# First two weight chunks issued from ScalarE's queue; squares of the first norm later; the eighth square kept beside the sum

## The chip, the cores and the metric

The kernel runs on one core of one Trainium2 chip. The metric is the device time of one execution in microseconds (us), from outside the program; the profile's span, from the first to the last instruction, is a little shorter. Each engine (TensorE = PE, with its weight loads listed apart as PEld; VectorE = DVE; ScalarE = ACT; GpSimd = POOL; SyncE = SP) runs its own list of instructions in order and waits on semaphores for the others. DMA queues are fed by an issuing instruction on an engine; in the kernel before, all of them stand on SP.

## What is computed

Two layers of a decoder trunk on 256 tokens of width 1024, float32. Each layer normalises x, multiplies it with one wide matrix, runs three token mixers, merges them through gates, and ends with a gated feed-forward block behind a second norm:

```python
def _rms(x, g):
    y = xf * lax.rsqrt(jnp.mean(xf * xf, axis=-1, keepdims=True) + EPS)
    return (y * g.astype(jnp.float32)).astype(x.dtype)

xn = _rms(x, norm_mix_g);  z = jnp.einsum('btd,dc->btc', xn, w_in)
...                        # mLSTM, sparse attention, differential attention, branch gates
x = x + jnp.einsum('btd,de->bte', merged, w_out)
xn = _rms(x, norm_ffn_g);  gu = jnp.einsum('btd,df->btf', xn, w_gate_up)
return x + jnp.einsum('btf,fd->btd', jax.nn.silu(g) * u, w_down)
```

So there are four norms in a run: the mixing norm and the feed-forward norm of each of the two layers. The first of them opens the program.

## The kernel before, in words

**Tiling.** x is held transposed: 8 blocks `x[0]` to `x[7]` of 128 features by 256 tokens, side by side in the tile `xs` (lines 485 and 486). Weights come in chunks of 128 by 1024 (`chunk`, lines 509 to 522), numbered here c0, c1, c2, ... in the order of use. A chunk is loaded into one of three `raw` buffers and split: ScalarE writes the rounded high part `whi`, VectorE the rest `wlo` (`split`, lines 524 to 526); three buffers each. The activations are split in the same way (`gained`, line 547, gives `xg` or `fx`). A product is then three matmul passes, hi by hi, hi by lo and lo by hi (`feat`, line 528), each with 256 columns; one chunk is 24 matmuls. A `raw` buffer is free for a next load when its `wlo` is done, so the load of c7 waits for the `wlo` of c4.

**Start.** The first layer's first two chunks and x are loaded in pieces (lines 602 to 620): x in four pieces of two blocks, c0 and c1 in halves of 512 columns, all eight from SP, alternating. `x_parts` splits the blocks, `split` the halves. `first_pair` (line 630) runs 26 small matmuls on zeros and then the 48 matmuls of c0 and c1 in the order in which pieces become ready. Then c2, c3, ... follow in full chunks.

**Norm.** Matmuls run on `x * gain`; the factor 1/rms is applied afterwards to what the matmuls gave. `norm` (line 551) computes it: the squares of the eight blocks are summed in `acc` (tile `nacc`); PE transposes `acc` (tokens to partitions), VectorE reduces it to `rcol`, GpSimd takes the power -1/2, VectorE copies it out (`rc`), PE transposes that back and ScalarE writes it as `rB`. In the first norm (lines 566 to 573) the squares are two ScalarE instructions of 1024 columns, held behind the `wlo` of c1 in the planned order (line 568), and three VectorE additions. In the other three (lines 575 to 581) each block is squared by ScalarE and added by GpSimd, 7 additions one after the other. What a matmul of the first layer left in PSUM is read out as `pad` (line 792), which needs `rB`; until then the PSUM buffer is held.

**Order.** The code records all operations, and a list scheduler (`Order.schedule`, line 206) with a cost table puts them into one order, per engine; each engine runs its list as it stands. `S.after(view)` holds the next operations in that planning behind the writers of the view. `PLACED` (line 416) lists tiles and spacers that are laid out first in SBUF.

Of the kernel before, what the change touches and what calls it, by code (L numbers as in the profile page):

```python
# [11 lines left out]
F32 = mybir.dt.float32  # L12
F32R = mybir.dt.float32r
BF16 = mybir.dt.bfloat16
AF = mybir.ActivationFunctionType
OP = mybir.AluOpType
AX = mybir.AxisListType.X
# [100 lines left out]
class Order:  # L118
# [87 lines left out]
    def schedule(self):  # L206
        ops = self.ops
# [39 lines left out]
        while len(out) < len(ops):  # L247
            for e in ENGINES:
                if e not in stale:
                    continue  # L250
                c = []
                full = set()
                for p, i in sorted(avail[e]):
                    tag = ops[i].bases[0].tag
                    if tag in full:
                        continue
                    at = start(ops[i], t_eng[e])
                    if at is not None:
                        c.append((at, p, i))
                    if e == "sync":  # L260
                        full.add(tag)
                if c:
                    t = min(c)[0] + SLACK[e]
                    picks[e] = min((p, i, at) for at, p, i in c if at <= t)
                else:
                    picks[e] = None
            stale.clear()
            c = [(picks[e][2], e) for e in ENGINES if picks[e]]
            if not c:
                raise RuntimeError("the order is stuck: " + repr([(e, [(ops[i].fn, [(b.name, b.slot, len(free[b.tag])) for b in ops[i].bases]) for _, i in sorted(avail[e])[:6]]) for e in ENGINES]))  # L270
            at, e = min(c)
            p, i, _ = picks[e]
            o = ops[i]
# [3 lines left out]
            for b in o.bases:  # L277
                if not b.slot:
                    free[b.tag].pop(0)
                    b.slot = True  # L280
                    stale.update(ENGINES)
            if e == "sync":
                dma = max(at, dma) + o.dur
                o.end, t_eng[e] = dma + DMA_LAT, at + DMA_ISSUE
            else:
                if e == "scalar":
                    fits = [f for f in TABLES if o.args[2] in f]
                    if fits and table not in fits:
                        table = fits[0]
                        at += 1.283  # L290
                o.end = t_eng[e] = at + o.dur
# [62 lines left out]
def cost(op, views):  # L354

    n = max(math.prod(v.shape[1:]) for v in views)
    psum = any(v.base.psum for v in views)
    if op.eng == "tensor":
        n = math.prod(views[0].shape[1:])
# [4 lines left out]
        if views[1].dtype == F32R:  # L364
            return max(n, 256) / 2400 + 0.0024
        return 0.216 if n <= 128 else 4 * n / 2400 + 0.0048
    if op.eng == "scalar":
        t = (0.05 if psum else 0.092) + n * 0.00084
        extra = [op.kw.get("scale"), op.kw.get("bias"), op.kw.get("accum_out")]
        return t + 0.093 * sum(isinstance(v, View) for v in extra)  # L370
# [23 lines left out]
T = 256  # L394
# [18 lines left out]
BR = (1, 2, 0)  # L413


PLACED = ("whi", "wlo", "nacc", 192, "xg", "y", "h", 192, "w", 224, "mqk", 192, "K1", 416)


def plan():
# [37 lines left out]
def kernel(ctx: ExitStack, tc: tile.TileContext, xT: bass.AP, wts: bass.AP, cst: bass.AP,  # L457
# [6 lines left out]
    S = Order(tc, sbuf, psum)  # L464
# [5 lines left out]
    def atps(shape):  # L470
        return S.tile(shape, F32, tag="at", name="at", bufs=4, psum=True)

    def tmp(shape, name="w"):
        return S.tile(shape, F32, tag="w", name=name, bufs=NW)
# [76 lines left out]
    def norm(gcol, wide, xg=None):  # L551

        first = xg is not None
        xg = xg or []
        acc = S.tile([128, T], F32, tag="nacc", name="nacc")
        for k in range(8 - len(xg)):
            g = gcol[:, k:k + 1]
            if not wide:
# [6 lines left out]
            xg.append(a)  # L565
        if first:
            sq = S.tile([128, 8 * T], F32, tag="y", name="sq8", bufs=3)
            with S.after(w_first[1][1]):
                for a in (0, 4 * T):
                    A.activation(sq[:, a:a + 4 * T], xs[:, 8 + a:8 + a + 4 * T], AF.Square)  # L570
            for n in (4 * T, 2 * T):
                V.tensor_add(sq[:, 0:n], sq[:, 0:n], sq[:, n:2 * n])
            V.tensor_add(acc, sq[:, 0:T], sq[:, T:2 * T])
        else:
            for k in range(8):
                if k == 0:
                    A.activation(acc, x[k], AF.Square)
                else:
                    sq = tmp([128, T], "nsq")
                    A.activation(sq, x[k], AF.Square)  # L580
                    G.tensor_add(acc, acc, sq)
        ps = atps([128, 2, 128])
        with S.gang():
            for t in range(2):
                PE.transpose(ps[:, t, :], acc[:, t * 128:(t + 1) * 128], ident)
        rcol = S.tile([128, 2], F32, tag="rcol", name="rcol", bufs=2)
        V.tensor_reduce(rcol, ps, axis=AX, op=OP.add)
        V.tensor_scalar(rcol, rcol, 1.0 / D, EPS, op0=OP.mult, op1=OP.add)
        rsqrt_cols(rcol, 2)
        rr = tmp([128, 2, 128], "rc")  # L590
# [11 lines left out]
    xg0, w_first = [], [chunk(0), chunk(0)]  # L602
    with S.early(10 ** 6):
        def load(i, a, b):
            SP.dma_start(w_first[i][0][:, a:b], w_first[i][3][:, a:b])

        def load_x(k, n):
            a = 8 + T * k if k else 0
# [150 lines left out]
                                       op0=OP.mult, op1=OP.subtract)  # L759

    for li in range(L):
        widx[0] = 2 if li == 0 else 0
        c = col[li]
        r = row[li] = S.tile([128, R_N], F32, tag="row", name="row")
        ps_first = mmps([128, 2, T]) if li == 0 else None
        if li == 0:
            first_pair(ps_first)
        xg, rcol, rB = norm(c[:, C_NM:C_NM + 8], False, xg0 if li == 0 else None)
        if li:
            SP.dma_start(r, rows[li:li + 1, :].to_broadcast([128, R_N]))  # L770
# [7 lines left out]
        for fp in range(4):  # L778
            if li == 0 and fp == 0:
                ps = ps_first  # L780
            else:
                ps = mmps([128, 2, T])
                for j in range(2):
                    w = chunk(li)
                    for k in range(8):
                        feat(ps[:, j, :], w, k * 128, xg[k], k == 0, k == 7)
            qk = S.tile([128, 2, T], F32, tag="mqk", name="mqk", bufs=4)
# [496 lines left out]
```

## Time and profile before

| what | value |
|---|---|
| device time, median of 3 runs | 909.11 us (903.57 to 916.03) |
| time of the profiled execution | 910.13 us |
| its span | 908.0 us |
| PE busy | 897.8 us, 7162 matmuls |
| DVE, ACT, POOL busy | 675.6, 536.0, 111.6 us |
| granted TensorE clock | 1.000 |

The profiled execution lies 1.02 us above the median of the three, and its time is 2.1 us more than its span. The first real matmul starts 6.28 us into the span. Of the last 108 us PE is busy for 104.25; what is left is the end of the kernel behind its last matmul, mostly. PE's records are pipelined matmuls that overlap: their durations of some 280 ns are longer than the distance from one to the next.

### The profile page before, as it was taken

Reading aid. Unit: us, or ns where it says so; the run is one execution under the profiler, and the core shown is the slowest. Engines: PE = TensorE matmul, PEld = TensorE weight load, DVE = VectorE, ACT = ScalarE, POOL = GpSimd, SP = SyncE. Lnnn points to the kernel's source line nnn. Section 1 sums busy time; section 2 is a strip of 40 time slices with the busy share of each in tenths; the row PEclk is TensorE's granted clock in tenths of the full one; section 3 lists DMA queues with packets and bytes.
Section 4 is the critical chain, followed back from the end, with each engine's and each line's share of the span. In section 5 each row is a group of like instructions: output and inputs, shape, how many; then the busy total and the mean of one; then the engine's idle time right before and its main releaser. Section 6 shows DMA issues by size and latency. Waiting matters only on the chain.

```text
span 908.0 us, 18059 instructions
## 1 busy us (share of the span) xinstructions
PE 897.8 (99%) x7162; PEld 857.3 (94%) x7162; DVE 675.6 (74%) x1276; ACT 536.0 (59%) x928; POOL 111.6 (12%) x142
## 2 busy tenths in 40 slices
PE   9999999999999999999999999999999999999998
PEld 8978779999999999999999787899999999999998
DVE  6999989766896666665578899897669866666553
ACT  6786677765465444444457857687654655545442
POOL 0333342300021000000110221312000300000000
PEclk9999999999999999999999999999999999999999
DMA  8665524356555555555665554433555555555663
GB/s 260 197 200 183 165 91 126 123 176 196 196 187 186 187 186 187 186 176 189 190 188 181 181 186 141 138 110 125 186 190 194 198 185 191 197 195 189 197 210 102
DMA packets 46453, 160.50 MB, mean 177 GB/s; under 512 B 5408, under 2 KB 6560, under 8 KB 46368
## 3 DMA queue, kind: packets, MB, share of 16 engines
q1 hardware_dynamic: 46368, 159.34, 53.8%
q8 instruction: 56, 0.92, 0.4%
q14 instruction: 29, 0.24, 0.1%
HBM read 158.27 MB, written 1.05 MB: 175 GB/s over the span
## 4 chain that ended last, share of the span: by engine, by line
PE 88%; DVE 6%; POOL 2%; DMA 2%; issue 1%; ACT 1%; ACTq 0%; DVEq 0%
PE mm L323 83%; PE at L323 5%; DVE e L323 2%; DVE wlo L323 2%; POOL s L323 2%; DMA raw<-in_wts_dram 1%; ACT whi L323 1%; DMA x<-in_xT_dram 0%; DVE zr L323 0%; DVE cv L323 0%; DVE y L323 0%; DVE s L323 0%; DVE rot L323 0%; DVE pad L323 0%; DVE xg L323 0%
## 5 line engine op out<-in xcount | busy, mean ns | idle before, releaser
L323 ACT ACTIVATE whi<-raw 128x1024 fp32r<-128x1024 f32 (+3 forms) x304 | 316.5, 1042 | 316.6 <-PE mm L323 150.3
L323 DVE TENSOR_TENSOR wlo<-raw,whi 128x1024 fp32r<-128x1024 f32 (+3 forms) x304 | 364.5, 1200 | 170.8 <-ACT whi L323 169.0
L323 PE MATMUL mm<-fx,whi 128*128 128x256 f32 x1408 | 245.1, 279 | 0.0
L323 PEld LDWEIGHTS mm<-fx,whi 128*128 128x128 f32 x1408 | 214.7, 189 | 0.0
L323 PE MATMUL mm<-fx,wlo 128*128 128x256 f32 x704 | 195.9, 279 | 0.0
L323 PE MATMUL mm<-xg,whi 128*128 128x256 f32 x1024 | 181.4, 280 | 0.3 <-ACT whi L323 0.3
L323 PEld LDWEIGHTS mm<-xg,whi 128*128 128x128 f32 x1024 | 155.4, 188 | 1.7 <-issue 0.7
L323 PE MATMUL mm<-whi,xg 128*128 128x512 f32 (+2 forms) x512 | 149.1, 372 | 1.1 <-DVE pad L323 1.1
L323 PE MATMUL mm<-xg,wlo 128*128 128x256 f32 x512 | 142.5, 281 | 0.8 <-DVE wlo L323 0.8
L323 PEld LDWEIGHTS mm<-fx,wlo 128*128 128x128 f32 x704 | 132.0, 188 | 0.0
L323 PE MATMUL mm<-h,whi 128*128 128x256 f32 x704 | 122.1, 279 | 0.0
L323 PEld LDWEIGHTS mm<-whi,xg 128*128 128x128 f32 x512 | 92.0, 188 | 17.3 <-issue 1.5
L323 PEld LDWEIGHTS mm<-h,whi 128*128 128x128 f32 x704 | 107.4, 189 | 0.0
L323 PE MATMUL mm<-h,wlo 128*128 128x256 f32 x352 | 98.1, 279 | 0.0
L323 PEld LDWEIGHTS mm<-xg,wlo 128*128 128x128 f32 x512 | 95.8, 188 | 1.1 <-DVE wlo L323 1.1
L323 PE MATMUL mm<-wlo,xg 128*128 128x512 f32 (+2 forms) x256 | 94.9, 371 | 0.0
L323 PEld LDWEIGHTS mm<-h,wlo 128*128 128x128 f32 x352 | 66.1, 188 | 0.0
L323 PE MATMUL mm<-y,whi 128*128 128x256 f32 x384 | 65.4, 276 | 0.0
L323 POOL TENSOR_TENSOR nacc<-nacc,nsq 128x256 f32<-128x256 f32 x21 | 20.2, 962 | 348.0 <-ACT nsq L323 210.1
L323 PEld LDWEIGHTS mm<-y,whi 128*128 128x128 f32 x384 | 57.8, 188 | 0.0
L323 PEld LDWEIGHTS mm<-wlo,xg 128*128 128x128 f32 x256 | 48.1, 188 | 7.3
L323 PE MATMUL mm<-y,wlo 128*128 128x256 f32 x192 | 53.0, 276 | 0.0
(199 smaller groups left out, 1083.6 us busy)
## 6 DMA issues: line engine op xcount, KB each, us to landing
raw<-in_wts_dram SPq DMA_DIRECT2D x278, 512.0 KB, 3.4
raw<-in_wts_dram SPq DMA_DIRECT2D x16, 384.0 KB, 3.8
raw<-in_wts_dram SPq DMA_DIRECT2D x4, 498.0 KB, 4.0
raw<-in_wts_dram SPq DMA_DIRECT2D x4, 256.0 KB, 4.8
out_dram<-x SPq DMA_DIRECT2D x8, 128.0 KB, 3.4
row<-in_rows_dram SPq DMA_DIRECT2D x2, 388.0 KB, 5.3
x<-in_xT_dram SPq DMA_DIRECT2D x3, 256.0 KB, 5.0
raw<-in_wts_dram SPq DMA_DIRECT2D x2, 332.0 KB, 3.0
```

What stands on the lines that cost most here:

```text
L323: getattr(getattr(nc, o.eng), o.fn)(*args, **kw)
```

## The change

It does four things. (1) The halves of c0 and c1 are issued from ScalarE's queue (`A.dma_start`), and SP issues x alone; the scheduler is taught that a DMA can stand on another engine than SP. (2) c2 and c3 are declared ahead of the first norm (`w_next`), and the two squares of that norm are planned behind the `whi` of c2 and of c3. (3) `nacc` is now 128 x 2 x 256, a temporary tile; in the first norm the last addition of 256 columns is left out and the addition before it writes `nacc`; in the other three the eighth square is written by ScalarE into the second half, so GpSimd adds 6 times. Four transposes instead of two bring it to the reduction, which runs over 512 columns instead of 256. (4) `nacc` is no longer in `PLACED`, so the tiles behind it lie 1024 bytes lower in each partition.

```diff
-PLACED = ("whi", "wlo", "nacc", 192, "xg", "y", "h", 192, "w", 224, "mqk", 192, "K1", 416)
+PLACED = ("whi", "wlo", 192, "xg", "y", "h", 192, "w", 224, "mqk", 192, "K1", 416)
...
-        acc = S.tile([128, T], F32, tag="nacc", name="nacc")
+        acc = tmp([128, 2, T], "nacc")
...
-            with S.after(w_first[1][1]):
-                for a in (0, 4 * T):
-                    A.activation(sq[:, a:a + 4 * T], xs[:, 8 + a:8 + a + 4 * T], AF.Square)
-            for n in (4 * T, 2 * T):
-                V.tensor_add(sq[:, 0:n], sq[:, 0:n], sq[:, n:2 * n])
-            V.tensor_add(acc, sq[:, 0:T], sq[:, T:2 * T])
+            for a in range(2):
+                with S.after(w_next[a][0]):
+                    A.activation(sq[:, 4 * a * T:4 * (a + 1) * T], xs[:, 8 + 4 * a * T:8 + 4 * (a + 1) * T], AF.Square)
+            V.tensor_add(sq[:, 0:4 * T], sq[:, 0:4 * T], sq[:, 4 * T:8 * T])
+            V.tensor_add(acc.rearrange("p a t -> p (a t)"), sq[:, 0:2 * T], sq[:, 2 * T:4 * T])
         else:
             for k in range(8):
-                if k == 0:
-                    A.activation(acc, x[k], AF.Square)
+                if k in (0, 7):
+                    A.activation(acc[:, k // 7, :], x[k], AF.Square)
                 else:
                     sq = tmp([128, T], "nsq")
                     A.activation(sq, x[k], AF.Square)
-                    G.tensor_add(acc, acc, sq)
+                    G.tensor_add(acc[:, 0, :], acc[:, 0, :], sq)
-        ps = atps([128, 2, 128])
+        ps = atps([128, 2, 2, 128])
         with S.gang():
-            for t in range(2):
-                PE.transpose(ps[:, t, :], acc[:, t * 128:(t + 1) * 128], ident)
+            for i in range(2):
+                for t in range(2):
+                    PE.transpose(ps[:, t, i, :], acc[:, i, t * 128:(t + 1) * 128], ident)
...
-            SP.dma_start(w_first[i][0][:, a:b], w_first[i][3][:, a:b])
+            A.dma_start(w_first[i][0][:, a:b], w_first[i][3][:, a:b])
```

**ScalarE's list at its start**, before and after. `xg` are the high parts of the blocks of x, `whi` those of weights (512 columns: halves of c0 and c1). Before:

```order
L323 ACT_TABLE_LOAD
L323 ACTIVATE warm<-warm 128x1
L323 ACTIVATE xg<-x 128x256 x2
L323 ACTIVATE whi<-raw 128x512
L323 ACTIVATE xg<-x 128x256 x2
L323 ACTIVATE whi<-raw 128x512 x2
L323 ACTIVATE xg<-x 128x256 x2
L323 ACTIVATE whi<-raw 128x512
L323 ACTIVATE xg<-x 128x256 x2
L323 ACTIVATE sq_68<-x 128x1024
L323 ACTIVATE whi<-raw 128x1024
L323 ACTIVATE sq_68<-x 128x1024
```

After:

```order
L323 DMA raw<-in_wts_dram 128x512 x4
L323 ACT_TABLE_LOAD
L323 ACTIVATE warm<-warm 128x1
L323 ACTIVATE whi<-raw 128x512
L323 ACTIVATE xg<-x 128x256 x2
...
L323 ACTIVATE whi<-raw 128x512
L323 ACTIVATE xg<-x 128x256 x2
L323 ACTIVATE whi<-raw 128x1024
L323 ACTIVATE sq_67<-x 128x1024
L323 ACTIVATE whi<-raw 128x1024
L323 ACTIVATE sq_67<-x 128x1024
```

Four DMA issues stand ahead of the table load; each half of a chunk is split ahead of the two blocks of x that it was behind; and each square has moved one whole `whi` back, behind those of c2 and c3.

**VectorE's list around the first norm**, from the `wlo` of c2 on (all `wlo` here are whole chunks, in the order c2, c3, c4, c5). Before:

```order
L323 TENSOR_TENSOR wlo<-raw,whi 128x1024
L323 TENSOR_TENSOR sq_68<-sq_68 128x1024
L323 TENSOR_TENSOR wlo<-raw,whi 128x1024 x2
L323 TENSOR_TENSOR sq_68<-sq_68 128x512
L323 TENSOR_TENSOR nacc<-sq_68 128x256
L323 TENSOR_TENSOR wlo<-raw,whi 128x1024
L323 TENSOR_REDUCE rcol<-at 128x2
```

After:

```order
L323 TENSOR_TENSOR wlo<-raw,whi 128x1024 x2
L323 TENSOR_TENSOR sq_67<-sq_67 128x1024
L323 TENSOR_TENSOR wlo<-raw,whi 128x1024
L323 TENSOR_TENSOR nacc<-sq_67 128x512
L323 TENSOR_TENSOR wlo<-raw,whi 128x1024
L323 TENSOR_REDUCE rcol<-at 128x2
```

The first addition of squares has moved from behind the `wlo` of c2 to behind that of c3, just ahead of that of c4, and one addition is gone.

On PE the transposes of the first norm's `nacc` stand 4 matmuls further back than before (behind the first matmul of c4), those of `rc` 5 matmuls further forward, so that 27 matmuls lie between the two instead of 36. In the two feed-forward norms the transposes of `nacc` stand 7 matmuls further forward, in the mixing norm of layer 1 five. Apart from the four norms and the start, every engine's list is the same, names aside.

## Rows read from the trace of the kernel before

**Rows 1.** Page: the span, and busy time of each engine.
```profile
span 908.0 us, 18059 instructions
PE 897.8 (99%) x7162; PEld 857.3 (94%) x7162; DVE 675.6 (74%) x1276; ACT 536.0 (59%) x928; POOL 111.6 (12%) x142
```

**Rows 2.** Waits of PE: engine and tile, waited for; us in total, times, longest.
```profile
PE at L323 <- DVE zr L323: 2.0, 2, 1.8
PE mm L323 <- DVE pad L323: 1.1, 1, 1.1
PE mm L323 <- DVE wlo L323: 0.8, 1, 0.8
```

**Rows 3.** Chain that ended last, in order of time: start us, us, what.
```profile
10.36 4.63 DMA raw<-in_wts_dram
...
17.46 5.81 DMA raw<-in_wts_dram
...
35.18 20.06 PE mm L323 x114
...
105.96 1.14 PE at L323 x16
```

**Rows 4.** Tile x: SP's issues, ns min/median/max, first and last start.
```profile
L323 SPq DMA_DIRECT2D x<-in_xT_dram x4: 387/428/449, 0.7 to 4.1; - x4
```

**Rows 5.** Windows: length, busy us of engines (count), clock, DMA share, GB/s.
```profile
2.00:3.00 1.00, 1.00 (x7) 0.69 (x6) 0.00 (x0) 0.21 (x2) 0.00 (x0) 1.00 0.67 156
...
5.00:6.00 1.00, 0.95 (x9) 0.59 (x6) 0.66 (x2) 1.00 (x3) 0.00 (x0) 1.00 1.04 399
```

**Rows 6.** Timeline of ScalarE: start, us, operation, count, idle before and its releaser.
```profile
0.72 1.28 ACT L323 ACT_TABLE_LOAD   x1 [0.72 <-PEq L1273]
...
4.79 0.91 ACT L323 ACTIVATE xg<-x 128x256 fp32r<-128x256 f32 x2 [2.57 <-DMA x<-in_xT_dram]
5.61 0.61 ACT L323 ACTIVATE whi<-raw 128x512 fp32r<-128x512 f32 x1
...
11.27 1.05 ACT L323 ACTIVATE whi<-raw 128x1024 fp32r<-128x1024 f32 x1
...
13.51 1.06 ACT L323 ACTIVATE whi<-raw 128x1024 fp32r<-128x1024 f32 x1 [0.24 <-DMA raw<-in_wts_dram]
```

**Rows 7.** Timeline of VectorE, from c2's low part to the first pad.
```profile
12.35 1.22 DVE L323 TENSOR_TENSOR wlo<-raw,whi 128x1024 fp32r<-128x1024 f32 x1 [0.80 <-ACT whi L323]
13.50 1.22 DVE L323 TENSOR_TENSOR sq<-sq 128x1024 f32<-128x1024 f32 x1
...
16.20 1.23 DVE L323 TENSOR_TENSOR wlo<-raw,whi 128x1024 fp32r<-128x1024 f32 x1 [0.35 <-ACT whi L323]
...
18.07 0.42 DVE L323 TENSOR_TENSOR nacc<-sq 128x256 f32<-128x256 f32 x1
...
20.79 0.42 DVE L323 TENSOR_REDUCE rcol<-at 128x2 f32<-128x256 f32 x1
...
25.60 0.42 DVE L323 TENSOR_TENSOR pad<-mm,rB 128x256 f32<-128x256 f32 x1
```

**Rows 8.** Timeline of PE: c2's first low pass, and the first norm's transposes.
```profile
13.63 0.39 PE L323 MATMUL mm<-xg,wlo 128*128 128x256 f32 x1 [0.76 <-DVE wlo L323]
...
18.64 0.38 PE L323 MATMUL at<-K,nacc 128*128 128x128 f32 x2
...
23.51 0.66 PE L323 MATMUL at<-K,rc 128*128 128x128 f32 x4 [0.39 <-DVE rc L323]
```

**Rows 9.** Timeline of PE around a later norm (feed-forward, layer 0).
```profile
277.30 0.44 PE L323 MATMUL at<-K,nacc 128*128 128x128 f32 x2
277.49 0.48 PE L323 MATMUL mm<-fx,whi 128*128 128x256 f32 x2
...
280.99 0.60 PE L323 MATMUL at<-K,rc 128*128 128x128 f32 x4
281.34 0.36 PE L323 MATMUL mm<-fx,whi 128*128 128x256 f32 x1
```

More of the change, by code (lines that the diff above doesn't have):

```diff
@@ L259, in schedule @@
                         c.append((at, p, i))
-                    if e == "sync":
+                    if ops[i].fn == "dma_start":
                         full.add(tag)
@@ L281, in schedule @@
                     stale.update(ENGINES)
-            if e == "sync":
+            if o.fn == "dma_start":
                 dma = max(at, dma) + o.dur
@@ L366, in cost @@
         return 0.216 if n <= 128 else 4 * n / 2400 + 0.0048
-    if op.eng == "scalar":
+    if op.eng == "scalar" and op.fn != "dma_start":
         t = (0.05 if psum else 0.092) + n * 0.00084
@@ L580, in norm @@
                     A.activation(sq, x[k], AF.Square)
-                    G.tensor_add(acc, acc, sq)
-        ps = atps([128, 2, 128])
+                    G.tensor_add(acc[:, 0, :], acc[:, 0, :], sq)
+        ps = atps([128, 2, 2, 128])
         with S.gang():
-            for t in range(2):
-                PE.transpose(ps[:, t, :], acc[:, t * 128:(t + 1) * 128], ident)
+            for i in range(2):
+                for t in range(2):
+                    PE.transpose(ps[:, t, i, :], acc[:, i, t * 128:(t + 1) * 128], ident)
         rcol = S.tile([128, 2], F32, tag="rcol", name="rcol", bufs=2)
-        V.tensor_reduce(rcol, ps, axis=AX, op=OP.add)
+        V.tensor_reduce(rcol, ps.rearrange("p t a c -> p t (a c)"), axis=AX, op=OP.add)
         V.tensor_scalar(rcol, rcol, 1.0 / D, EPS, op0=OP.mult, op1=OP.add)
@@ L761 @@
     for li in range(L):
-        widx[0] = 2 if li == 0 else 0
+        if li:
+            widx[0] = 0
         c = col[li]
@@ L767 @@
             first_pair(ps_first)
+            w_next = [chunk(0), chunk(0)]
         xg, rcol, rB = norm(c[:, C_NM:C_NM + 8], False, xg0 if li == 0 else None)
@@ L783 @@
                 for j in range(2):
-                    w = chunk(li)
+                    w = w_next[j] if li == 0 and fp == 1 else chunk(li)
                     for k in range(8):
```

## The prediction

> **What bounds the kernel now.** I first read the page. TensorE is busy for 897.8 of 908.0 us [rows 1], so all that a better order could ever win is the other 10.2 us, 1.1% of the time. A measurement of this kernel can tell about 2% (18.2 us) from no change, and the three runs of before alone lie 12.5 us apart. No hidden wait can therefore make this kernel faster by 2%: the questions are only which way the few microseconds at the start go, and whether something makes the matmuls themselves slower.
>
> Next I read PE's waits. In the stretch that the change touches there are two: 0.8 us for the `wlo` of c2, which ends at 13.63 [rows 8], and 1.1 us for a `pad`, which ends at 35.18 [rows 2, 3]. The 1.8 us for `zr` comes at 132 us, behind a stretch of VectorE and GpSimd work that PE itself started at 105.96 [rows 2, 3]; a shift of PE at 35.18 goes through to the end of the kernel undiminished.
>
> The chain of waits says which of the two counts. Up to 35.18 it does not run over PE. It runs over loads and splits: the load of c4 (4.63 us from 10.36), c4's split, the load of c7 (5.81 us from 17.46), c7's split, and then VectorE's `pad` [rows 3]. A load of c7 starts when c4's `wlo` is done: 16.20 plus 1.23 is 17.43 [rows 7]. Reading this, a PE that is early at 13.63 only waits longer at 35.18. **The time at 35.18 is set by when VectorE finishes c4's `wlo`.**
>
> **Part 1, the issues.** SP's four x issues run from 0.7 to 4.1 us because four weight issues of a like 0.43 us stand between them [rows 4]. Taken apart, the last of each kind is issued near 2.1, up to 2 us earlier. But the DMA engines are full soon after: 156 GB/s in the third microsecond, 399 in the sixth, with a share of 1.04 [rows 5]. What the earlier issue wins can only be in the ramp. The trace has no second queue, so I bound it. Best case: the first half chunk lands beside x's first piece at 4.79, where ScalarE's wait for x ended. Worst case: the two share the engines and both land when, before, both had landed, which is by 5.61, where ScalarE took the half chunk without a wait [rows 6]. So ScalarE starts between 4.79 and 5.61, that is 0 to 0.8 us later than before.
>
> Here the Trainium skill speaks against the change: "DMA: Bandwidth & Descriptors", section "Issuing engines are not separate DMA queues", says that DMAs from several engines run on the same 16 DMA engines and interleave, and that only the sequencer's issue time is saved; its section on queues, rings and completion order has each DMA engine go round between queues packet by packet. By that rule the first piece of x lands together with the first half chunk, the late case. The saturated row agrees; the sharing itself no run here shows.
>
> The four issues on ScalarE take some 4 x 0.43 = 1.7 us (SP's price; ScalarE's is not in the trace). With the 1.28 us table load behind them ScalarE is ready near 0.72 + 1.7 + 1.28 = 3.7, before anything lands [rows 4, 6]. They cost nothing; if an issue took twice as long, ScalarE would be ready at 5.4 and they would cost up to 0.6.
>
> **Part 2, the new order at the start.** ScalarE does the same 12 instructions (8 blocks, 4 halves) until the last block. Before, c2's `whi` came at 11.27 because a square of 1.05 us stood ahead of it [rows 6]; now it starts at 10.3 to 11.1. c2's `wlo` then ends 0.1 to 0.9 us earlier than 13.57, and so PE's wait of 0.76 shrinks to 0 to 0.7. This is what the move of the squares gives.
>
> **Part 3, what the squares run into.** They now follow the `whi` of c2 and c3, and VectorE's first addition of them, 1.22 us, has moved to just ahead of c4's `wlo` [rows 7]. c3's `whi` starts on its load, at 13.51 [rows 6], and ends at 14.57; the second square ends near 15.6, and c4's `whi` near 16.6. On VectorE c3's `wlo` ends at 14.6 + 1.2 = 15.8, the addition, waiting for the square, at 17.0, c4's `wlo` at 18.2. Before it ended at 17.43: **c4's `wlo` is 0.8 us later**, 1.4 at most if the pieces land late. Behind it on VectorE wait the sum, c5's `wlo` and the reduction; on SP waits the load of c7.
>
> **Part 4, the sum and its way back.** One addition of 512 columns writes `nacc`; its 0.69 us is between the 0.42 us of 256 columns and the 1.22 of 1024 [rows 7]. `nacc` is ready at 18.9 where it was at 18.49. Before, 43 matmuls lay between 13.63 and 18.64 [rows 8], 0.117 us each; PE would now want it 47 after 12.7 to 13.5, at 18.2 to 19.0, so a new wait of up to 0.8 us is likely there. Then c5's `wlo` (1.2) and the reduction over twice the columns (0.42, up to 0.84): 20.8. From the reduction's start to the transposes of `rc` it took 23.51 - 20.79 = 2.7 us [rows 7, 8]; now 20.2 + 2.7 + 0.2 = 23.1. PE comes there after 27 instead of 36 matmuls, at 19.0 + 0.45 + 3.15 = 22.6, and waits 0.5 us (0.39 before). It has then done 5 fewer matmuls (0.6 us) 0.4 us earlier: 0.2 us behind, which the 1.1 us of slack in front of 35.18 covers.
>
> **Part 5, at 35.18.** c7's load starts near 18.2. With the two latencies of the chain, 4.63 and 5.81 [rows 3], it lands at 22.8 to 24.0; before, at 23.27. In the middle that is 0.15 later; with the late start (18.8) and the long latency, 1.4 later. It can't help more than some 0.9: `rc` at 23.1 still has to become `rB` before the first `pad`, which stood at 25.60 [rows 7] behind c7's `wlo`. I take +0.3, from -0.9 to +1.4.
>
> **Part 6, the three later norms.** There PE is the bound. Two transposes took 0.19 us until the next matmul, four 0.35 [rows 9]: +0.16 each, 0.5 us together, 0.3 if transposes that come without a short wait for GpSimd's sum are cheaper. GpSimd's missing addition and the earlier sum win nothing, since no wait of PE in the table of waits stands there [rows 2].
>
> **The sum.** 910.13 + 0.3 + 0.5 = 910.9 for a profiled execution, with bounds -0.6 and +1.9. The profiled execution of before lies 1.02 above the median, so the median comes to 909.9 us. It is a shift of less than 0.1%, far inside the scatter of the runs.
>
> **The rivals.**
>
> *A, the start pays.* The two queues fill the ramp, c7's load takes the short latency, and `pad` comes up to 0.9 us earlier: 910.13 - 0.9 + 0.3 is 909.5, a median of 908.5. For it speaks the row of 156 GB/s; against it, that c4's `wlo` would have to keep its time despite the addition put in front.
>
> *B, the late start.* x shares the engines with the weights, everything at the start is 0.8 us later, c4's `wlo` ends at 18.8 and `pad` is 1.4 late: 910.13 + 1.4 + 0.5 = 912.0, a median of 911.0. This is what the page's interleaving makes of it. For it speaks the share of 1.04 [rows 5], against it that the engines are not full before the fifth microsecond.
>
> *C, slower by more than 2%: the new places in SBUF.* All tiles behind `wlo` move by 1024 bytes. If TensorE's reads depended on that, 18.2 us over 7162 matmuls is 2.5 ns each, from 0.117 to 0.1195 us; from there on it decides. It would be seen in every stage, not at the start, and the time would be 928 us or more. Against it: VectorE's splits of c2 and c4, in different buffers of each of the three kinds, took 1.22 and 1.23 us [rows 7], so the address did not show there.
>
> That the change does nothing at all is part of the forecast: the loads are hidden or bound by bandwidth, and the time does not move.
>
> **How the numbers follow.** The forecast (a shift at the end between -0.5 and +1.5 us) has 0.56, A 0.2, B 0.2, C 0.03, and 0.01 stays for a gain of 2% that no row explains. A and B end within 2% as the forecast does. So: faster 0.01, same 0.96, slower 0.03. The cases A to B span only 908.5 to 911.0; the runs of before scatter from 5.5 below to 6.9 above their median, and a new median will share in that. The range goes from 903.5 (A and a scatter of 5) to 916.0 (B and a scatter of 5).
>
> **What the changed profile would show.** Right: ScalarE idle until its first `whi` at 4.8 to 5.6; c2's `wlo` ends before 13.5; the addition of squares stands between c3's and c4's `wlo` and c4's ends near 18.2; PE waits for `nacc`, at about 19; the wait for `pad` near 35 has grown to 1.0 to 2.5 us; the first matmul behind it starts between 34.3 and 36.6; four transposes at each later norm. Wrong: if the whole of PE's steady stretch (300 to 400 us, no idle) has another number of matmuls per microsecond, it is C. If the matmul behind `pad` starts before 34.3, the chain of loads was not what I took it for. If there is a wait of PE of over 1 us at a later norm, part 6 falls.

## The result, and the profile after

The changed kernel takes 903.46 us (median of 21 runs, 902.74 to 904.49) against 909.65 us (902.23 to 916.91) of the kernel before beside it: medians 6.2 us apart, 0.7%. The ratio is 0.995, 95% interval 0.9933 to 0.9967; it and all ratios below leave out executions that are over 1.5% longer than the fastest of their kernel, here the five longest of before. The forecast was 909.9 us, between 903.5 and 916.0. The ratio is below one beyond its interval, and the forecast had no such gain in it.

The single times say more than the medians. The 21 runs of before lie on three levels: six at 902.2 to 903.6, nine at 908.8 to 910.7, six at 915.2 to 916.9. Nothing lies between the levels, which are some 6.6 us apart. All 21 runs of the changed kernel lie on the lowest. So the change did not make the best case of before faster (its own mean is 903.5, that of before's lowest six 903.0): it took the two upper levels away.

The page of the changed kernel: span, and busy time of each engine. It answers to [rows 1].

```profile
span 901.2 us, 18068 instructions
PE 891.4 (99%) x7170; PEld 851.1 (94%) x7170; DVE 675.0 (75%) x1275; ACT 535.8 (59%) x928; POOL 110.3 (12%) x139
```

PE does 8 instructions more (the transposes) and is busy for 6.4 us less, almost all of the 6.8 us by which the span shrinks. PE still idles for some 10 us. The waits that have gone or come are small beside that; the matmuls themselves have become quicker.

The chain of waits that ended last shows where. First the changed kernel (start us, us, what); the first four rows answer to [rows 3]:

```profile
1.65 6.92 DMA raw<-in_wts_dram
11.37 4.79 DMA raw<-in_wts_dram
18.62 5.28 DMA raw<-in_wts_dram
35.82 13.07 PE mm L323 x84
...
280.53 177.51 PE mm L323 x1566
...
722.73 174.79 PE mm L323 x1542
```

The same chain of the kernel before, at the feed-forward (FFN) blocks of layers 0 and 1, behind the norm's `rc` transposes:

```profile
281.59 183.64 PE mm L323 x1558
...
730.94 173.32 PE mm L323 x1529
```

Divide time by count. After: 177.51 / 1566 and 174.79 / 1542, 0.1134 us a matmul in both layers. Before: 173.32 / 1529 is 0.1134 as well, but 183.64 / 1558 is 0.1179. In layer 0 of that execution each matmul took 4.5 ns more, for 184 us without one wait: 7.0 us in all. Windows, first of before (one in each layer), then of after: length; busy us of PE, PEld, DVE, ACT and POOL, with counts; granted clock, DMA share, GB/s:

```profile
300.00:400.00 100.00, 100.00 (x851) 100.00 (x850) 62.52 (x90) 48.37 (x71) 0.00 (x0) 1.00 0.56 184
800.00:880.00 80.00, 80.00 (x708) 80.00 (x708) 48.78 (x67) 36.72 (x49) 0.00 (x0) 1.00 0.61 196
```

```profile
300.00:400.00 100.00, 100.00 (x885) 100.00 (x884) 64.80 (x93) 50.47 (x74) 0.00 (x0) 1.00 0.60 193
```

851 matmuls against 885 in layer 0, PE "busy" for 100.00 us in both, the granted clock 1.00 (the 2.4 GHz level) in both. A busy share of 100% hides a pace that is 4% slower. **PE has two lasting paces here, 113 and 118 ns a matmul.** The profiled executions of the middle level (that of before, and two further down) each have one of the two FFN stretches at the slower pace, and the 17 profiled on the lowest level have none. That both are slow on the upper level follows from its distance; no execution of it was profiled. In shorter stretches, between 150 and 170 us for one, the slower pace occurs in every kernel, the changed one too. Below, "the slow pace" means that of an FFN stretch.

The start went much as forecast. Waits of PE in the changed kernel, the answer to [rows 2]:

```profile
PE at L323 <- DVE zr L323: 2.0, 2, 1.8
PE mm L323 <- ACT xg L323: 1.2, 1, 1.2
...
PE mm L323 <- DVE pad L323: 0.5, 1, 0.5
...
PE at L323 <- DVE rc L323: 0.4, 1, 0.4
```

Its ScalarE timeline (start, us, operation, count, idle before and releaser), the answer to [rows 6]:

```profile
0.72 1.86 ACTq L323 DMA_DIRECT2D raw<-in_wts_dram  x4
2.61 1.28 ACT L323 ACT_TABLE_LOAD   x1 [2.61 <-issue]
...
5.64 0.63 ACT L323 ACTIVATE whi<-raw 128x512 fp32r<-128x512 f32 x1 [1.53 <-DMA raw<-in_wts_dram]
...
11.25 1.04 ACT L323 ACTIVATE whi<-raw 128x1024 fp32r<-128x1024 f32 x1
...
16.27 1.06 ACT L323 ACTIVATE whi<-raw 128x1024 fp32r<-128x1024 f32 x1 [0.55 <-DMA raw<-in_wts_dram]
```

Its VectorE timeline, the answer to [rows 7]:

```profile
12.32 1.23 DVE L323 TENSOR_TENSOR wlo<-raw,whi 128x1024 fp32r<-128x1024 f32 x1
14.80 1.23 DVE L323 TENSOR_TENSOR wlo<-raw,whi 128x1024 fp32r<-128x1024 f32 x1 [1.25 <-ACT whi L323]
15.94 1.22 DVE L323 TENSOR_TENSOR sq<-sq 128x1024 f32<-128x1024 f32 x1
17.36 1.23 DVE L323 TENSOR_TENSOR wlo<-raw,whi 128x1024 fp32r<-128x1024 f32 x1 [0.20 <-ACT whi L323]
18.50 0.69 DVE L323 TENSOR_TENSOR nacc<-sq 128x512 f32<-128x512 f32 x1
...
20.68 0.68 DVE L323 TENSOR_REDUCE rcol<-at 128x2 f32<-128x512 f32 x1
...
26.23 0.42 DVE L323 TENSOR_TENSOR pad<-mm,rB 128x256 f32<-128x256 f32 x1
```

And its PE timeline at the first norm and at the FFN norm of layer 0, the answer to [rows 8, 9]:

```profile
19.70 0.60 PE L323 MATMUL at<-K,nacc 128*128 128x128 f32 x4
...
23.80 0.66 PE L323 MATMUL at<-K,rc 128*128 128x128 f32 x4 [0.42 <-DVE rc L323]
```

```profile
276.86 0.60 PE L323 MATMUL at<-K,nacc 128*128 128x128 f32 x4
277.21 0.36 PE L323 MATMUL mm<-fx,whi 128*128 128x256 f32 x1
...
279.94 0.60 PE L323 MATMUL at<-K,rc 128*128 128x128 f32 x4
```

ScalarE takes its first half chunk at 5.64, just behind the late end of what was allowed; the addition of squares stands ahead of c4's `wlo`, which ends at 18.59; behind `pad` PE goes on at 35.82, 0.64 us later than the 35.18 of [rows 3].

### The profile page after: what moved, and what is told of

Same layout as the page of the kernel before. It is cut to its first block, busy times and chain, and to the rows that moved or that the text cites. A ratio compares the mean times of both kernels' runs of the same rounds, so it can differ in the third digit from the quotient of the medians.

```text
span 901.2 us, 18068 instructions
## 1 busy us (share of the span) xinstructions
PE 891.4 (99%) x7170; PEld 851.1 (94%) x7170; DVE 675.0 (75%) x1275; ACT 535.8 (59%) x928; POOL 110.3 (12%) x139
## 4 chain that ended last, share of the span: by engine, by line
PE 87%; DVE 7%; DMA 2%; POOL 2%; ACT 1%; issue 1%; ACTq 0%; DVEq 0%
PE mm L323 83%; PE at L323 5%; DVE e L323 2%; DVE wlo L323 2%; DMA raw<-in_wts_dram 2%; POOL s L323 2%; ACT whi L323 1%; DVE zr L323 0%; DVE cv L323 0%; DVE y L323 0%; DVE s L323 0%; DVE rot L323 0%; DVE pad L323 0%; DVE mn L323 0%; DVE zir L323 0%
## 5 line engine op out<-in xcount | busy, mean ns | idle before, releaser
L323 ACT ACTIVATE whi<-raw 128x1024 fp32r<-128x1024 f32 (+3 forms) x304 | 317.1, 1044 | 308.9 <-PE mm L323 224.2
L323 DVE TENSOR_TENSOR wlo<-raw,whi 128x1024 fp32r<-128x1024 f32 (+3 forms) x304 | 364.7, 1200 | 168.5 <-ACT whi L323 166.3
L323 PE MATMUL mm<-fx,whi 128*128 128x256 f32 x1408 | 240.3, 276 | 0.0
L323 PEld LDWEIGHTS mm<-fx,whi 128*128 128x128 f32 x1408 | 211.9, 188 | 0.0
L323 PE MATMUL mm<-fx,wlo 128*128 128x256 f32 x704 | 194.3, 276 | 0.0
L323 PE MATMUL mm<-xg,whi 128*128 128x256 f32 x1024 | 182.7, 280 | 1.2 <-ACT xg L323 1.2
L323 PEld LDWEIGHTS mm<-xg,whi 128*128 128x128 f32 x1024 | 155.9, 188 | 3.3 <-ACT xg L323 1.7
L323 PE MATMUL mm<-whi,xg 128*128 128x512 f32 (+2 forms) x512 | 149.1, 372 | 0.5 <-DVE pad L323 0.5
L323 PE MATMUL mm<-xg,wlo 128*128 128x256 f32 x512 | 142.1, 280 | 0.0
L323 PEld LDWEIGHTS mm<-fx,wlo 128*128 128x128 f32 x704 | 132.1, 188 | 0.0
L323 PE MATMUL mm<-h,whi 128*128 128x256 f32 x704 | 119.8, 276 | 0.0
L323 PEld LDWEIGHTS mm<-whi,xg 128*128 128x128 f32 x512 | 92.0, 188 | 16.7 <-issue 1.5
L323 PEld LDWEIGHTS mm<-h,whi 128*128 128x128 f32 x704 | 105.8, 188 | 0.0
L323 PE MATMUL mm<-h,wlo 128*128 128x256 f32 x352 | 97.2, 276 | 0.0
L323 PEld LDWEIGHTS mm<-xg,wlo 128*128 128x128 f32 x512 | 95.8, 188 | 0.0
L323 PE MATMUL mm<-wlo,xg 128*128 128x512 f32 (+2 forms) x256 | 94.9, 371 | 0.0
L323 PEld LDWEIGHTS mm<-h,wlo 128*128 128x128 f32 x352 | 66.1, 188 | 0.0
L323 PE MATMUL mm<-y,whi 128*128 128x256 f32 x384 | 65.4, 276 | 0.0
L323 POOL TENSOR_TENSOR nacc<-nacc,nsq 128x256 f32<-128x256 f32 x18 | 17.6, 979 | 331.4 <-ACT nsq L323 198.1
L323 PEld LDWEIGHTS mm<-y,whi 128*128 128x128 f32 x384 | 57.7, 188 | 0.0
L323 PEld LDWEIGHTS mm<-wlo,xg 128*128 128x128 f32 x256 | 48.1, 188 | 7.3
L323 PE MATMUL mm<-y,wlo 128*128 128x256 f32 x192 | 53.0, 276 | 0.0
```

The source lines that it names most:

```text
L323: getattr(getattr(nc, o.eng), o.fn)(*args, **kw)
```

## The experiments

Two questions: which part of the change keeps the slow pace away, and what the rest of the change costs. Each set ran on one chip with the kernel before beside it. "High" below means above 908 us; no execution of any kernel lies between 905.1 and 908.7.

**First set: parts of the change one by one** (before beside it: 909.68 us, 11 of 16 high). Theory N said that the new order at the later norms keeps the slow pace away, theory P that the places in SBUF do. N had two forms: theory W, that PE's short wait for GpSimd's sum lets the slow pace in, and theory K, that it is where the `rc` transposes cut the matmuls.

The eighth square alone; `nacc` moves, all other tiles keep their places:

```diff
+PLACED = ("whi", "wlo", 1024, 192, "xg", "y", "h", 192, "w", 224, "mqk", 192, "K1", 416)
...
+        acc = tmp([128, T] if first else [128, 2, T], "nacc")
...
+                if k in (0, 7):
+                    A.activation(acc[:, k // 7, :], x[k], AF.Square)
```

> Before, with the eighth square beside the sum in the three later norms alone (6 additions on GpSimd, 4 transposes); start, queues, first norm and the places of all other tiles in SBUF as before. In before's profile PE runs at 0.1175 us per matmul from the feed-forward norm of layer 0 (277 us) to the next norm (465 us), and at 0.1133 in the same stretch of layer 1; in the changed kernel at 0.1133 in both. Theory N (the norms' transposes throw PE into the slow rate, and the eighth square ends it): every run at 902.5 to 903.5, none near 909.6 or 916, and both stretches at 0.1133. Theory P (it is the 1024 bytes by which the tiles moved): the runs stay spread over 903, 909.6 and 916 as in before.

902.17 us (902.04 to 902.53, 4 runs, none high), ratio 0.9925 [0.9895, 0.9955].

The places alone, every engine's list as before:

```diff
-PLACED = ("whi", "wlo", "nacc", 192, "xg", "y", "h", 192, "w", 224, "mqk", 192, "K1", 416)
+PLACED = ("whi", "wlo", 192, "xg", "y", "h", 192, "w", 224, "mqk", 192, "K1", 416)
```

> Before with the one edit that nacc is not laid out in front, so that all tiles behind the low parts lie 1024 bytes lower; every engine's list is that of before. Theory P: all runs at 902 to 903.6. Theory N: spread over 903, 909.6 and 916 as in before, median near 909.6.

902.81 us (902.32 to 902.93, 5 runs, none high), ratio 0.9937 [0.9905, 0.997].

The changed kernel with seven additions and two transposes again in the later norms:

```diff
-                if k in (0, 7):
-                    A.activation(acc[:, k // 7, :], x[k], AF.Square)
+                if k == 0:
+                    A.activation(acc[:, 0, :], x[k], AF.Square)
```

> The changed kernel with the sum of all eight squares on GpSimd again in the three later norms (7 additions, 2 transposes); its start, its queues, its first norm and its places in SBUF stay. Theory N: the runs spread again over three levels, here near 903.5, 910 and 916.5, and the profile shows 0.1175 us per matmul in those feed-forward stretches that are slow. Theory P: all runs stay at 902.7 to 904.5.

904.32 us (903.26 to 904.92, 11 runs, none high), ratio 0.9955 [0.9925, 0.9986].

The kernel before with PE's later transposes moved back by some eight matmuls, by another planned duration (on VectorE the reduction behind them moves back by one `wlo`; no place changes):

```diff
-        op.dur *= MARGIN.get(eng, 1.0) if self.margin else 1.0
+        op.dur = op.dur * (MARGIN.get(eng, 1.0) if self.margin else 1.0) if eng != 'gpsimd' or outs[0].base.name != 'nacc' else 1.5
```

> Before with GpSimd's additions of squares planned at 1.5 us each, which moves only PE's transposes of the later norms: those of nacc come 8 matmuls later, so that PE no longer waits for GpSimd there, and those of rc later still, again between the two passes over the same high weights, as in before. Theory N has two forms. W (PE's wait of 0.2 us for the sum starts the slow rate): all runs near 903. K (it is where the rc transposes cut the three passes of a block; the state after them lasts): three levels as in before, since the cut is the same.

903.06 us (902.7 to 903.39, 5 runs, none high), ratio 0.9934 [0.9908, 0.9961].

So none of the four was high, though no edit is common to them; the first three have `nacc` at another address, the last has not. Each theory that named one part alone was contradicted by another kernel.

**Second set: the start, and which place** (before beside it: 902.95 us, 6 of 35 high). The queue edit alone:

```diff
-            SP.dma_start(w_first[i][0][:, a:b], w_first[i][3][:, a:b])
+            A.dma_start(w_first[i][0][:, a:b], w_first[i][3][:, a:b])
```

> The kernel before with only the first two weight chunks' pieces on ScalarE's queue: every row on TensorE, all tiles' places and the three later norms stay as before, only the first 20 us differ. Theory P (the order of TensorE's rows and the places in SBUF together allow the slow pace of the FFN stretches, wherever the start lies): the times spread again over some 13 us, levels near 903.5, 910 and 917, median near 910. Theory T (the slow pace hangs on finer timing than that): all runs within 2 us of 903.5. For the start both theories say the same by the terms of the prediction: the first norm's transposes come 0.3 to 0.8 us later than the 35.18 us of before.

903.89 us (903.64 to 910.46), 2 of 12 high. With the order at the later norms and the places of before, the slow pace is still there.

nacc alone elsewhere, an empty space in its place; and then nacc in its place, the tiles behind it 1,024 bytes further up:

```diff
+PLACED = ("whi", "wlo", 1024, 192, "xg", "y", "h", 192, "w", 224, "mqk", 192, "K1", 416)
...
+PLACED = ("whi", "wlo", "nacc", 1216, "xg", "y", "h", 192, "w", 224, "mqk", 192, "K1", 416)
```

> The kernel before with the norms' running sum nacc at another address and an empty space of the same 1,024 bytes left in its old place: the rows of all five engines and the addresses of whi, wlo, xg, y, h and the others stay. If the address of the tile that the norms transpose matters by itself: all runs within 1.5 us of 902.8, as with e4_place. If it is the addresses of the tiles that the matmuls read (y and h in the FFN stretches, which e4_place moved by 1,024 bytes): levels 903, 909.5 and 916 as before, median near 909.7.

902.75 us (902.04 to 903.65), 0 of 12 high.

> The kernel before with nacc, whi and wlo in their places and the tiles behind (xg, y, h, w, mqk, K1) 1,024 bytes further up: the rows of all five engines stay. If the addresses of the tiles that the matmuls read matter: all runs within 1.5 us of 902.8. If it is nacc's address that matters: levels 903, 909.5 and 916 as before, median near 909.7. If any moved tile at all takes the slow pace away, this kernel and the one that moves nacc alone both stay near 902.8.

902.84 us (902.02 to 909.65), 3 of 12 high. Moving the tiles that the FFN matmuls read (`y`, `h`) did not take the slow pace away. Where before is high in 6 of 35, none of 12 comes by chance about once in ten times, so p_nacc says little by itself.

> The changed kernel again, beside the other three, as a yardstick for the start: 903.5 (902.7 to 904.5) in all runs if its FFN stretches never take the slow pace; a run near 910 would show that it can. Against the run that has only the queue edit it tells what the later squares cost or give: by the prediction's terms under 0.5 us either way.

903.74 us (903.05 to 904.03), 0 of 10 high. Here the kernel before was mostly on its lowest level, and **the change gains nothing**: ratio 0.9995 [0.9974, 1.0016].

**Third set** (before: 902.98 us, 9 of 35 high).

```diff
-        op.dur *= MARGIN.get(eng, 1.0) if self.margin else 1.0
+        op.dur = op.dur * (MARGIN.get(eng, 1.0) if self.margin else 1.0) if eng != 'gpsimd' or outs[0].base.name != 'nacc' else 1.1
```

> The kernel before with the planner's time for GpSimd's additions into nacc set to 1.1 us, so that in the three later norms the two nacc transposes stand a few rows earlier on TensorE and wait longer for GpSimd, and the rc transposes stand between two blocks (wlo, rc, whi x2), as in the changed kernel; all places in SBUF as before. Theory W (the wait for GpSimd's sum is what lets the slow pace in): levels 903, 910 and 916 in about the same shares as the kernel before beside it. Theory K (it is the cut of the rc transposes between the two whi passes): all runs near 903.0, up to 1 us more for the longer waits.

903.82 us (903.37 to 905.1), 0 of 12 high. The expectation described this kernel wrongly: its nacc transposes stand four matmuls later than in before, not earlier, and its trace has no wait for GpSimd's sum at the later norms. So it tells nothing for K against W; it is one more kernel without the wait and without a slow FFN stretch. But its profiled execution, the 905.1 us, holds the slower pace for some 30 us behind the later mixing norm, where PE waited 0.2 us for `rc`. The row of the chain there, and the same row of the run with the queue edit:

```profile
463.19 29.23 PE mm L323 x233
```

```profile
463.04 28.33 PE mm L323 x233
```

> nacc alone at another address, once more, beside the kernel before on the same chip. If nacc's address is what matters: no run above 904.5, however many of before's lie near 910 and 916. If it is the addresses of the other tiles: levels in the same shares as before.

902.87 us (901.98 to 903.16), 0 of 12 high.

> The kernel before with only the eighth square beside the sum, in the three later norms, again: 902.2 (901.6 to 902.8) in all runs, 0.7 us under the lowest level of before, since the trace of its first run shows about 0.1 us won at each later norm and no wait for GpSimd. A run near 909 would show that the slow pace is still to be had with this order of rows and the places of before.

902.54 us (901.77 to 902.88), 0 of 12 high, ratio 0.9981 [0.9961, 1.0].

> The changed kernel beside the run with the eighth square alone: 903.6, that is 1.2 to 1.6 us above that one, which is the price of the start with two queues and later squares; no run near 910.

903.64 us (902.74 to 904.13), 0 of 10 high, ratio 0.9993 [0.9971, 1.0014]. The run with the eighth square alone is 1.1 us faster beside it: **it is the best version here**, ahead of both kernels, though only 0.4 us ahead of before in this set, where the interval reaches 1.0.

**Fourth set: order against address** (before: 903.24 us, 1 of 24 high). The eighth square with the sums at nacc's old address; the later transposes again; nacc moved by 96 bytes and nothing else:

```diff
+        both = S.tile([128, 2, T], F32, tag="nacc", name="nacc")
+        acc = both[:, 0, :] if first else both
...
+PLACED = ("whi", "wlo", 96, "nacc", 96, "xg", "y", "h", 192, "w", 224, "mqk", 192, "K1", 416)
```

> The rows of the run with the eighth square alone, but the two partial sums in one tile that begins at nacc's old address (the tiles behind it lie 1,024 bytes further up, which by itself did not matter). If it is the address of nacc alone that allows the slow pace: some runs near 909, in the same shares as the kernel before beside it. If the changed order at the norms (no wait for GpSimd, rc between two blocks) keeps it away by itself: all runs 902.3 (901.7 to 903.2).

902.57 us (902.17 to 904.3), 0 of 11 high.

> The kernel before with the nacc transposes a few rows later, so that TensorE does not wait for GpSimd at the later norms; nacc at its old address. If the address alone decides: some runs near 909.5, in the shares of the kernel before beside it. If the order at the norms does: all near 903.0 (902.4 to 903.6).

903.1 us (902.48 to 903.88), 0 of 11 high.

> The kernel before with nacc alone moved by 96 bytes, into the gap behind it; all rows and all other places as before. If any other address of nacc takes the slow pace away: all runs near 902.8. If the slow pace comes back in the shares of the kernel before beside it, 96 bytes are not enough to leave it, and it is the region or nacc's distance to other tiles by more than that.

909.37 us (902.68 to 909.79), 6 of 7 high, where the kernel before beside it had 1 of 24. So nacc's old address is nothing special: with before's order another address can be far worse. Since before itself was almost never high in this set, the other two runs say little by themselves.

**Fifth set: the wait alone** (before: 909.53 us, 17 of 29 high). The narrowest test: all rows and all places of before, in the same order on every engine, but GpSimd's last addition is so short that its sum is ready in time. It leaves 240 of the 256 columns of the eighth square out of the sum, so the values behind the norms differ. No run separates that from the missing wait at the same rows; h15_late lost the wait with the sum whole, but with rows moved.

```diff
-                    G.tensor_add(acc, acc, sq)
+                    n = 256 if k < 7 else 16
+                    G.tensor_add(acc[:, 0:n], acc[:, 0:n], sq[:, 0:n])
...
+        if eng == 'gpsimd' and outs[0].base.name == 'nacc':
+            op.dur = (0.15 + 256 * 0.0021) * (MARGIN['gpsimd'] if self.margin else 1.0)
```

> The kernel before with GpSimd's last addition of each later norm cut from 256 to 16 columns (the other 240 columns of the eighth square are left out of the sum): every row on every engine and all places as before, but GpSimd's sum is done earlier, so that TensorE's nacc transposes need not wait for it. Theory W (that wait, some 0.14 us at each FFN norm, lets the slow pace in): all runs near 902.6 (902.0 to 903.3), however many of before's lie near 910 and 916. Theory K (the order of TensorE's rows at the norm lets it in): levels in the shares of the kernel before beside it.

902.82 us (901.76 to 909.42), **1 of 13 high** against 17 of 29 of before beside it.

> The same short last addition, with nacc moved by 96 bytes as in the run that took the slow pace in 6 of 7 executions. Theory W: all runs near 902.6. Theory K: levels in the shares of p_off2 beside it.

902.08 us (901.7 to 902.51), **0 of 12 high**.

> The kernel before with nacc moved by 96 bytes, again, as the yardstick for the run with the short last addition at these places. If the shares go with the places: most runs near 909.4 again. If they go with the chip: another share.

909.53 us (902.61 to 909.91), **9 of 12 high**: the yardstick for the run above, same rows, same places, with the wait.

The wait as the trace of before shows it, in the table of waits of the weight loads (PEld) between 270 and 300 us; the same row stands in the trace of p_off2, and none in that of n_short:

```profile
PEld at L323 <- POOL nacc L323: 0.2, 1, 0.2
```

The profiled execution of p_off2 has the slow pace in layer 1, and that of n_short, its one execution above 908 us, in layer 0. Their chains, p_off2 first (L323 and L325 are the same line of the code, two lines further down in n_short):

```profile
281.34 176.48 PE mm L323 x1557
...
723.71 180.10 PE mm L323 x1529
```

```profile
281.26 183.50 PE mm L325 x1558
...
730.24 173.32 PE mm L325 x1529
```

Four rows, two paces: 0.1133 and 0.1178, 0.1178 and 0.1134. The windows of p_off2 show the pace with a granted clock of 1.00 again, 885 matmuls in 100 us of layer 0 but 682 in 80 us of layer 1 (885 would give 708):

```profile
300.00:400.00 100.00, 100.00 (x885) 100.00 (x884) 65.07 (x92) 50.24 (x74) 0.00 (x0) 1.00 0.60 193
...
800.00:880.00 80.00, 80.00 (x682) 80.00 (x681) 46.72 (x63) 35.29 (x47) 0.00 (x0) 1.00 0.61 190
```

**All runs together**, by whether PE waits for GpSimd's sum at the FFN norms (read from the one profile of each run):

| kernels | wait | above 908 us |
|---|---|---|
| before, six sets | yes | 15/21, 11/16, 6/35, 9/35, 1/24, 17/29 |
| queue edit; other tiles moved; nacc moved by 96 bytes, twice | yes | 2/12, 3/12, 6/7, 9/12 |
| nacc elsewhere (e4_place, p_nacc twice); e5_sum8 | yes | 0/5, 0/24, 0/11 |
| changed kernel, three sets | no | 0/41 |
| eighth square alone, twice, and at the old address | no | 0/16, 0/11 |
| later transposes (h15 twice, h11) | no | 0/16, 0/12 |
| short last addition, two places | no | 1/13, 0/12 |

Without the wait 1 execution of 121 is high; with it 79 of 243. Only the sets in which before is often high weigh much: in the first comparison, the first and the fifth set it is 1 of 55 without the wait, and 43 of 66 of before. What follows: taking the wait away took the slow pace almost away in the fifth set, with rows and places unchanged. It is not the only door, since n_short has one execution above 908 us without a wait. The places matter beside it: nacc 96 bytes further gave 6 of 7 beside 1 of 24, and three kernels with the wait and nacc elsewhere gave 0 of 40.

**What stays open.** The same program, rows and places alike, was high in 1 of 24 executions in one set and in 17 of 29 in another, on the same chip; no run tells what differs. Nor does any run show what inside TensorE holds a pace for 180 us, or how an address of a tile that only the norm touches bears on it. How the wait does it is open too: it does not set the pace of the matmuls right behind it. Rows of the chain between the `nacc` and the `rc` transposes of layer 0's FFN norm, of n_short_off (no wait, never high) and of e4_place (wait, never high):

```profile
276.99 3.42 PE mm L325 x29
```

```profile
277.47 3.31 PE mm L323 x29
```

The one without the wait is at the slower pace there, 0.118 us a matmul against 0.114; the choice that lasts falls behind `rc`. And since e4_place and e5_sum8 keep the wait and were never high beside a before that was high in 11 of 16, the new places of the changed kernel may have been enough by themselves; losing the wait may be a second reason. Which of its parts kept the changed kernel at the quicker pace is therefore not shown, only that several do it alone.

**What the rest of the change costs.** A row of the chain that all kernels have, the 120 matmuls in 27.48 us near 70 us, marks how late the start made PE. In before, in the run with the queue edit alone, and in the changed kernel:

```profile
70.69 27.48 PE mm L323 x120
```

```profile
71.39 27.48 PE mm L323 x120
```

```profile
71.27 27.48 PE mm L323 x120
```

Over 15 profiles with the start of before this row begins at 69.65 to 71.33 us (mean 70.50); over the five with the issues on ScalarE (the queue edit alone, the changed kernel three times, e5_sum8) at 70.78 to 72.52 (mean 71.57). The start costs 1.1 us. The queue edit alone has 0.9 of it in its one profile, and its executions below 908 us lie as far above those of before beside it (medians 903.85 and 902.91). From that row to the end of the span, without a slow stretch, seven profiles with the later norms of before, wait and all, take 830.24 to 830.49 us, six with the eighth square beside the sum 829.93 to 830.17 (901.2 - 71.27 = 829.93 for the changed kernel): the later norms win 0.2 us. The eighth square wins a little more outside the span: an execution takes 1.73 to 1.86 us longer than its span in the six runs that have it, and 2.07 to 2.18 us in all others. What passes in these 0.3 us no run shows.

## Why the prediction was wrong

**What bounds the kernel: the step that failed.** "TensorE is busy for 897.8 of 908.0 us [rows 1], so all that a better order could ever win is the other 10.2 us, 1.1% of the time." The busy time was taken as fixed work. It was 891.4 us after, for more matmuls. In the prediction's terms, the sum has no term for PE's pace in the FFN stretches: that was put at nothing, and it measured 7.0 us for one slow stretch. A count in a window would have shown it from the trace of before alone: 851 matmuls between 300 and 400 us, but 708 in the 80 us from 800, which is 885 in 100. (The 0.117 us that Part 4 takes for a matmul is not that pace: its 43 steps hold one of 0.23 us behind the wait, at 13.63; the others take 0.114.)

**The scatter: the second step that failed.** "It is a shift of less than 0.1%, far inside the scatter of the runs" takes 903.57, 909.11 and 916.03 for noise around a middle. They are three levels, by their distance with 0, 1 and 2 slow stretches, and a change can move the share of each. The range reached 5 us below A's 908.5, so the measured 903.46 fell 0.04 under its end; it was the size of the scatter that brought it so near, not a mechanism.

**Part 6: wrong in sign.** "GpSimd's missing addition and the earlier sum win nothing, since no wait of PE in the table of waits stands there [rows 2]." The wait stood in the table of the weight loads, 0.2 us at each of the two FFN norms; PE's own table has no row for it. Four transposes do cost 0.35 us, as forecast (276.86 to 277.21), but the three norms together came out 0.2 us cheaper in the span, and 0.3 outside it, instead of 0.5 dearer. And that small wait mattered far beyond its length: in the fifth set 1 of 25 executions without it was high, and 26 of 41 with it (before and p_off2).

**Rival C: the right sign to look for, in one direction only.** "Wrong: if the whole of PE's steady stretch (300 to 400 us, no idle) has another number of matmuls per microsecond, it is C." It has, 885 against 851. But C was priced as slower, in every stage, and by places alone. The places do matter (fourth set), only as a share of executions, and the moved tiles that the matmuls read were not the ones (p_shift).

**Parts 1 to 5: near in time, on the late side, and not always for the reason given.** ScalarE started at 5.64 (forecast 4.79 to 5.61). The Trainium skill, "DMA: Bandwidth & Descriptors", section "Issuing engines are not separate DMA queues", has DMAs of several engines interleave on the same 16 DMA engines and so spoke for the late case; the row at 5.64 agrees. ScalarE's issues took 1.86 us (forecast 1.7) and were free. c2's `whi` came at 11.25, no earlier than the 11.27 of [rows 6]: the late halves took what the square's move gave. PE waited 1.2 us for the first `xg` instead, and came late enough to find c2's `wlo` done. c4's `wlo` ended at 18.59 (18.2; 18.8 in rival B), but not because of the addition in front of it, as Part 3 has it: VectorE was idle for 0.20 us behind the addition, for c4's `whi`, and that had waited for its load, which began at 11.37 instead of 10.36. The reduction ended at 20.68 + 0.68 = 21.4 (20.8), `rc` stood at 23.80 (23.1). PE did not wait for `nacc`: it was later itself and came at 19.70. Behind `pad` it went on 0.64 later, between the forecast's +0.3 and B's +1.4. The wait there was 0.5 us, not 1.0 to 2.5: a PE that is late already waits less. Over several profiles the start costs 1.1 us, so rival B was nearer than the middle.

**The sum as it measured:** start +1.1, later norms -0.2, outside the span -0.3, and the slow pace gone. Counted by levels, the 21 runs of before had 9 + 2 x 6 = 21 slow stretches at 6.6 us, 6.6 us a run on average; less the 0.5 us by which the changed kernel's mean lies above before's lowest level, that is the gain. The other terms leave +0.6: beside the executions of before below 908 us the changed kernel's median lies 0.4 us higher in the first comparison and 0.8 in the second and third set.

## What to carry to other kernels

Times on separate levels are not noise: ask first how many levels there are, and count matmuls per window in a stretch without waits, since a busy share of 100% says nothing of the pace. Read the waits of the weight loads beside those of the matmuls; in this kernel a wait of 0.2 us ahead of a long stretch went with a cost far above itself. And when a change seems to win, run it where the old kernel is at its best too: here the issues on the second queue cost about a microsecond, and the eighth square alone was the version to keep.

## What the hardware showed that was not expected

Matmuls of 256 columns, fed without a wait at a granted clock of 1.00, ran at 113.4 or at 117.8 ns from start to start, and kept either pace for over 170 us. The Trainium skill, "TensorE: Matmul & The Clock Gate", section "Wait — 56ns, not 53.3ns?", gives columns over 2.4 GHz plus 2.5 ns for back-to-back matmuls; for 256 columns that is an estimate of 109.2 ns, below both paces of these traces, and the measured ones stand. Where such matmuls followed a group of transposes, in all 20 profiles, the starts went one of two ways: some went straight or within about four matmuls to 113 ns, often over one longer step of 122 or 123 ns, and the others stayed at 118 ns at least until the next transposes or wait. Of the 40 FFN norms in these profiles PE came to the `rc` transposes at 113 ns in 19, and left them at 113 ns in all of these; it came at 118 ns in 21 and left at 118 ns in 3, the three slow FFN stretches. With the eighth square's order (changed kernel, e1, e6) it came at 113 ns in 11 of 12, with the other orders in 8 of 28. That fits the changed kernel's even times, and it is a count over single profiles, not an experiment.
